# A hybrid decoder layer: the output products of an SSM pair are issued four steps after its first products

## The chip, the cores and the metric

The kernel runs on 1 core of one Trainium2 chip. The metric is the device time of one execution in microseconds (us), lower is better. Before the change the median of 3 runs is 755.06 us (754.26 to 757.27). The engines are named as the profile names them: PE is TensorE, DVE is VectorE, ACT is ScalarE, POOL is GpSimd, and SP is SyncE, which here only issues DMAs.

## What is computed

One layer on a sequence of 2048 rows of width 1024, in float32. The normalised input is multiplied with one matrix `w_in`, and three branches work on the columns of the result. A fourth set of columns gates them, and one more matrix closes the layer:

```python
h = rmsnorm(x, g_pre);  proj = h @ w_in
val, gate = proj[..., :MIX_W], proj[..., MIX_W:]
y_pool = pool_mixer(u_pool, w_pool, pool_scale)          # causal means over 2, 4, 8, 16 rows
y_ssm  = s5_mixer(u_ssm, a_re, a_im, log_dt, b_re, ...)   # 24 groups of 16 channels, 64 complex states each, then a gated unit
y_att  = memory_attention(q, mem, g_mem, w_kv)            # 4 heads into 256 memory tokens
y = concatenate([y_pool, y_ssm, y_att]) * silu(gate)
x = x + rmsnorm(y @ w_out, g_post)
```

The state-space mixer (SSM) is what the change is about. Its recurrence runs over time with a diagonal complex matrix. The kernel cuts time into 256 blocks of T = 8 rows: inside a block the output is a product with a small matrix, and from block to block a scan carries the state.

## The kernel before

Every float32 matrix product is made of three products of rounded parts: a value is split into a high part (an ACT copy to the rounded type) and a low part (a subtraction on DVE), and `mm3` (lines 162 to 165) issues high by high, high by low, low by high. `split` (lines 158 to 160) is the pair of ACT copy and DVE subtraction, so most splits carry line 159 or 160 in the profile.

**The phases.** First the input `x` is loaded transposed in four chunks of 512 rows, split, and multiplied with the SSM columns (tiles `pu`, written out as `us` to `ud`). Beside it run the keys and values of the memory (`pkv`, weights `wkv`), the tables of the SSM on POOL, the fold of the pooling weights (`pf`, `wpo`), and the row sums of squares of `x` (`rs_x`), from which a chain of small DVE instructions (`rs_sum` to the last `rs_y`) makes one scale per row. That scale is written to memory and read back as `rs_b` and `rs_ct`. Then come 52 projections, in two halves of the sequence: 13 weight tiles (2 queries `pjq`, 3 pooling `pjp`, 8 gates `pjg`) by 2 chunks in each half. Each is 24 matmuls of 128x512 into one of two banks of the tag `mm`. In the first half a weight tile of 1024x128 is loaded raw, split and also stored; in the second half the stored parts are loaded. Last come the gated unit (`pz`) and the output projection (`pout`).

**What sets the order.** The kernel is written in a tile language whose scheduler orders each engine's instructions by the program's order and by its own model of time. All engines then run their queues strictly in order. Work of the attention and of the SSM is cut into steps and put between projections: `tick_mid` (line 658) takes attention steps in the middle of a projection, `tick_end` takes one SSM step after each projection, at a pace of 1.02 steps. The 24 SSM groups are 12 pairs, and `ssm_schedule` (line 880) writes down the steps of each pair `b`, with `n = b + 1`:

```python
call((ssm_run1, b), (ssm_kernel_load, b), (ssm_build1, n))
call((ssm_kernel_split, b), (ssm_rotation, n))
call((ssm_input_load, n))
call((ssm_run2, b), (ssm_build2, n), (ssm_input_split, n), (ssm_output_split, n))
```

`ssm_run1` multiplies the split input `uh`, `ul` with `rh`, `rl` (tile `pa`) and takes the result through rotation and scan: `v`, `ax`, `gg`, `gs`, `h` alternate between ACT, DVE and POOL, and end in a split into `hh` (ACT) and `hl` (DVE). `ssm_run2` issues the output products: twelve matmuls into `py`, of `uh`, `ul` with `mh`, `ml` and of `hh`, `hl` with `oh`, `ol`. `ssm_build1` and `ssm_build2` make the matrices of the next pair (`ox`, `rt` on POOL; `pr` and `pk` on PE; `rh`, `rl`, `kst`). `ssm_kernel_load` reads `mraw` back from memory. The tiles `uh`, `ul`, `oh`, `ol`, `hh`, `hl` have one buffer each.

**Pools.** `t2k` (line 116) hands out temporaries of 2 KB per partition from 12 buffers; the row sums, the SSM steps and the attention use them. `w_tile` (line 586) loads a raw weight of 4 KB per partition into a buffer of its own, `wraw`, one in the pool `wp2` and, for two of the `wkv` weights, one in the pool of the first phase.

Of the kernel before, what the change touches and what calls it, by code (L numbers as in the profile page):

```python
# [10 lines left out]
F32 = mybir.dt.float32  # L11
F32R = mybir.dt.float32r
# [6 lines left out]
P = 128  # L19
D = 1024  # L20
SEQ = 2048
KT = D // P
# [11 lines left out]
NJ = SEQ // T  # L34
# [48 lines left out]
def hybrid_layer_kernel(  # L83
# [31 lines left out]
    def dma(o, i):  # L115
        nc.sync.dma_start(o, i)
# [11 lines left out]
    def t2k(name, shape=(P, CH), dtype=F32):  # L128
        return tmp.tile(list(shape), dtype, tag="t2k", name=name)
# [28 lines left out]
    def split(hi, lo, src, sub=dve):  # L158
        act.activation(hi, src, AF.Copy)  # L159
        sub.tensor_tensor(lo, src, hi.bitcast(F32), op=ALU.subtract)  # L160
# [122 lines left out]
    wp2 = p2.enter_context(tc.tile_pool(name="wp2", bufs=2, reuse_waits="tile"))  # L283
    p1 = ExitStack()
    ph1a = p1.enter_context(tc.tile_pool(name="ph1a", bufs=1))
# [247 lines left out]
    def mem_load():  # L533
        for k in range(KT):
            mr = xrp(f"mr{k}", (P, NMEM))
            dma(mr, memT[k * P:(k + 1) * P, :])
            m = big.tile([P, 2, NMEM], F32R, tag="xk", name=f"mhl{k}")
            act.activation(m[:, 0, :], mr, AF.Copy, scale=gmem[:, k:k + 1])
            dve.scalar_tensor_tensor(
                m[:, 1, :], mr, gmem[:, k:k + 1], m[:, 0, :].bitcast(F32), op0=ALU.mult, op1=ALU.subtract  # L540
            )
            mems.append(m)

    pkv = {}

    def kv_weight(m, raw=None):
        return w_tile(w_kv[:, m * P:(m + 1) * P], f"wkv{m}", raw)

    def kv_mm(m, w):
        if m % 2 == 0:  # L550
            pkv[m // 2] = mm_bank(f"pkv{m // 2}", (P, 2, NMEM))
        o = pkv[m // 2][:, m % 2, :]
        for k in range(KT):
            mm3(o, w[0][:, k, :], w[1][:, k, :], mems[k][:, 0, :], mems[k][:, 1, :], k == 0, k == KT - 1)
# [28 lines left out]
                dve.tensor_tensor(lo, src, hi.bitcast(F32), op=ALU.subtract)  # L583


    def w_tile(src, name, raw=None, spill=None, saved=None):
        wh = wp2.tile([P, KT, P], F32R, tag="whi", name=f"{name}_h")
        wl = wp2.tile([P, KT, P], F32R, tag="wlo", name=f"{name}_l")
        if saved is not None:
            dma(wh.bitcast(F32), saved[0])  # L590
            dma(wl.bitcast(F32), saved[1])
            return wh, wl
        wr = (raw or wp2).tile([P, KT, P], F32, tag="wraw", name=f"{name}_r", bufs=1)
        dma(wr, src.rearrange("(k p) m -> p k m", p=P))
        split(wh, wl, wr)
        if spill is not None:
            dma_later(spill[0], wh.bitcast(F32))
            dma_later(spill[1], wl.bitcast(F32))
        return wh, wl


    load_chunk(2, True)
    dma(gmem, g_mem)
    wkv = [kv_weight(0, ph1a)]
    mem_load()
    wkv.append(kv_weight(1))
    dma(cs, cst)
    u_mm(2, range(3), True)
    load_chunk(3, False)
    u_evac(2)  # L610
    kv_mm(0, wkv[0])
    wkv.append(kv_weight(2, ph1a))
    kv_mm(1, wkv[1])
    wkv.append(kv_weight(3))
    u_store(2)
# [48 lines left out]
    sp = ps_.enter_context(tc.tile_pool(name="sp", bufs=1, side="right", reuse_waits="tile"))  # L664
# [27 lines left out]
    def dma_later(o, i):  # L692

        deferred.append((o, i))
# [90 lines left out]
    def ssm_input_split(b, o):  # L785
        ur = o["ur"]
        pool.tensor_tensor(ur, ur, rs_ct.unsqueeze(1).broadcast_to([P, 2, NJ]), op=ALU.mult)
        uh = sp.tile([P, 2, NJ], F32R, tag="uh", name=f"uh{b}")
        ul = sp.tile([P, 2, NJ], F32R, tag="ul", name=f"ul{b}")
        split(uh, ul, ur)  # L790
        o["uh"], o["ul"] = uh, ul

# [85 lines left out]
    NB = NG // 2  # L878
    ssm_state = [dict() for _ in range(NB)]

    def ssm_schedule():
        def call(*fs):
            def go():
                for f, b in fs:
                    if b < NB:
                        f(b, ssm_state[b])

            ssm_q.append(go)

        call((ssm_input_load, 0), (ssm_build1, 0))  # L890
        call((ssm_build2, 0), (ssm_rotation, 0))
        call((ssm_input_split, 0), (ssm_output_split, 0))
        for b in range(NB):
            n = b + 1
            call((ssm_run1, b), (ssm_kernel_load, b), (ssm_build1, n))
            call((ssm_kernel_split, b), (ssm_rotation, n))
            call((ssm_input_load, n))
            call((ssm_run2, b), (ssm_build2, n), (ssm_input_split, n), (ssm_output_split, n))


    def q_split(ps, pr, c, qst):
# [346 lines left out]
    def prefetch(n):  # L1248
        if n < len(first_use) and first_use[n] not in weights:
            hf, i = first_use[n]  # L1250
            if hf not in tasks:
                tasks[hf] = half_tasks(hf)
            src, _, name = tasks[hf][i]
            if hf == 0:
                wsplit[i] = [dram.tile([P, KT, P], F32, name=f"ws{t}{i}") for t in "hl"]
                weights[hf, i] = w_tile(src, f"w{name}", spill=wsplit[i])
            else:
                weights[hf, i] = w_tile(src, f"w{name}", saved=wsplit[i])
# [15 lines left out]

    prefetch(0)
    ssm_schedule()
    for _ in range(3):
        ssm_q.popleft()()
# [3 lines left out]
    for n, (hf, i, cc) in enumerate(order):  # L1282
        if not (i == NTASK - 1 and cc == 0 or hf == 1 and i == 1 and cc == 0):
            prefetch(first_use.index((hf, i)) + 1)
        _, consume, name = tasks[hf][i]
# [121 lines left out]
```

## Time and profile before

| | before |
|---|---|
| median of 3 runs | 755.06 us (754.26 to 757.27) |
| the profiled execution | 754.54 us, of which the span from first to last instruction is 752.8 us |
| PE busy | 708.1 us, 94% of the span, 3449 matmuls |
| DVE busy | 525.7 us, 70% |
| ACT busy | 337.4 us, 45% |
| POOL busy | 364.1 us, 48% |
| granted TensorE clock, mean | 0.98 of 2.4 GHz |
| memory read and written | 81.68 MB and 38.68 MB |
| a load of half a row block of `x` (`rs_x`), or of one chunk piece (`xr`) | 256 KB, 32 of each |
| a raw projection weight (`wq_r`, `wp_r`, `wg_r`) | 512 KB, 13 of them |

PE has work in 94% of the span, so a gain must come from its idle time, from a higher granted clock, or from fewer matmuls. The change leaves the matmuls as they are. The table gives averages; which wait matters is read stage by stage.

### The profile page before, as it was taken

What the parts mean: (1) busy time and instruction counts of PE and PEld (TensorE: products, weight loads), DVE (VectorE), ACT (ScalarE), POOL (GpSimd) and SP (SyncE); (2) the same over time, 40 slices, a digit from 0 to 9 for tenths busy, and PEclk for the clock granted to TensorE, in tenths of its full rate; (3) what the DMA queues carried; (4) which work ended last, traced back from release to release, by engine and by line L of the source; (5) the groups of instructions that cost most, each with busy time, mean ns of one, the idle gap of its engine ahead of it and who ended that gap; (6) DMA issues with size and microseconds to landing.
All of it is one profiled execution on the core that took longest, in us unless ns stands there. A gap on an engine that the chain in (4) does not pass through costs nothing.

```text
span 752.8 us, 10077 instructions
## 1 busy us (share of the span) xinstructions
PE 708.1 (94%) x3449; PEld 575.9 (77%) x3449; DVE 525.7 (70%) x901; ACT 337.4 (45%) x731; POOL 364.1 (48%) x311
## 2 busy tenths in 40 slices
PE   6999787999979799888999999999999999999996
PEld 5788676887858588666888888888887888888885
DVE  4699594689889887978788978657606964343224
ACT  5675432557455453445555565447632524221111
POOL 0049852678758566846858488103042621421121
PEclk9999998999999899999999999999999999999999
DMA  7998985233333347482332324377725464330331
GB/s 252 309 328 270 336 288 156 98 108 126 121 114 119 112 150 247 161 280 83 122 107 71 121 81 154 134 224 275 226 80 192 130 199 123 113 126 14 112 113 56
DMA packets 95268, 121.03 MB, mean 161 GB/s; under 512 B 31585, under 2 KB 63025, under 8 KB 95217
## 3 DMA queue, kind: packets, MB, share of 16 engines
q1 hardware_dynamic: 82320, 90.08, 38.1%
q10 hardware_dynamic: 12896, 30.30, 10.6%
q8 instruction: 27, 0.44, 0.2%
q14 instruction: 25, 0.20, 0.1%
HBM read 81.68 MB, written 38.68 MB: 160 GB/s over the span
## 4 chain that ended last, share of the span: by engine, by line
PE 59%; DVE 13%; ACT 3%; issue 2%; DMA 1%; ACTq 0%; POOL 0%; DVEq 0%; POOLq 0%
PE pout L165 8%; PE pout L164 8%; PE pout L163 8%; PE pjg L163 5%; PE pjg L164 5%; PE pjg L165 5%; PE pz L163 2%; PE pz L165 2%; PE pz L164 2%; PE pjp L163 2%; PE pjp L164 2%; PE pjp L165 2%; DVE gg L847 2%; DMA ysd<-ys 1%; DVE yt L1007 1%
## 5 line engine op out<-in xcount | busy, mean ns | idle before, releaser
L163 PE MATMUL pjg<-xh,wg_h 128*128 128x512 f32 x256 | 103.6, 405 | 0.0
L164 PE MATMUL pout<-wol,yh 128*128 128x512 f32 (+1 forms) x264 | 102.0, 386 | 0.0
L164 PE MATMUL pjg<-xl,wg_h 128*128 128x512 f32 x256 | 101.9, 398 | 0.0
L165 PE MATMUL pjg<-xh,wg_l 128*128 128x512 f32 x256 | 101.7, 397 | 0.0
L163 PE MATMUL pout<-woh,yh 128*128 128x512 f32 (+1 forms) x264 | 101.6, 386 | 0.0
L165 PE MATMUL pout<-woh,yl 128*128 128x512 f32 (+1 forms) x264 | 101.2, 387 | 0.0
L1217 POOL TENSOR_TENSOR ov<-ov,xres 128x1024 f32<-128x1024 f32 x15 | 36.7, 2444 | 126.8 <-DVE ov L1216 105.0
L1213 ACT ACTIVATE ov<-pout 128x512 f32<-128x512 f32 x30 | 17.9, 596 | 105.3 <-PE pout L165 82.0
L163 PEld LDWEIGHTS pjg<-xh,wg_h 128*128 128x128 f32 x256 | 48.5, 189 | 12.8 <-issue 1.6
L164 PEld LDWEIGHTS pout<-wol,yh 128*128 128x128 f32 x264 | 49.5, 188 | 11.0
L163 PEld LDWEIGHTS pout<-woh,yh 128*128 128x128 f32 x264 | 49.5, 188 | 10.9
L165 PEld LDWEIGHTS pout<-woh,yl 128*128 128x128 f32 x264 | 49.5, 188 | 10.9
L165 PEld LDWEIGHTS pjg<-xh,wg_l 128*128 128x128 f32 x256 | 48.4, 189 | 11.3
L164 PEld LDWEIGHTS pjg<-xl,wg_h 128*128 128x128 f32 x256 | 48.7, 190 | 10.1
L160 POOL TENSOR_TENSOR yl<-yb,yh 128x512 fp32r<-128x512 f32 x20 | 26.9, 1375 | 60.6 <-ACT yh L159 39.7
L254 DVE SCALAR_TENSOR_TENSOR xl<-xr,gpre,xh 128x512 fp32r<-128x512 f32 x48 | 43.0, 908 | 18.7 <-ACT xh L253 18.6
L844 POOL TENSOR_TENSOR v<-v,ax 128x512 f32<-128x512 f32 x12 | 16.8, 1403 | 68.0 <-DVE ax L843 50.8
L253 ACT ACTIVATE xh<-xr,gpre 128x512 fp32r<-128x512 f32 x48 | 33.2, 715 | 32.4 <-DMA xr<-in_xT_dram 10.3
L163 PE MATMUL pu<-xh,wsh 128*128 128x512 f32 x96 | 39.0, 421 | 8.2 <-ACT wsh L159 6.8
L1185 DVE SCALAR_TENSOR_TENSOR ow<-ssq,ov 128x1 f32<-128x1 f32 x16 | 2.7, 168 | 54.7 <-ACT ov L1213 54.6
L163 PE MATMUL pjp<-xh,wp_h 128*128 128x512 f32 x96 | 39.0, 407 | 0.7 <-DVE gp L999 0.7
L164 PE MATMUL pu<-xl,wsh 128*128 128x512 f32 x96 | 38.7, 416 | 0.3 <-DVE xl L254 0.3
(300 smaller groups left out, 1929.3 us busy)
## 6 DMA issues: line engine op xcount, KB each, us to landing
xr<-in_xT_dram SPq DMA_DIRECT2D x32, 256.0 KB
rs_x<-in_x_dram SPq DMA_DIRECT2D x32, 256.0 KB
yd<-yt ACTq DMA_DIRECT2D x16, 512.0 KB
xres<-in_x_dram SPq DMA_DIRECT2D x16, 512.0 KB
out_dram<-ov SPq DMA_DIRECT2D x15, 512.0 KB
yb<-yd SPq DMA_DIRECT2D x20, 256.0 KB
wg_r<-in_w_in_dram SPq DMA_DIRECT2D x8, 512.0 KB
wsh<-wg_h ACTq DMA_DIRECT2D x8, 512.0 KB
```

The source lines that it names most:

```text
L160: sub.tensor_tensor(lo, src, hi.bitcast(F32), op=ALU.subtract)
L163: pe.matmul(ps, ahi, bhi, start=first, stop=False)
L164: pe.matmul(ps, ahi, blo, start=False, stop=False)
L165: pe.matmul(ps, alo, bhi, start=False, stop=last)
L253: act.activation(h, xr, AF.Copy, scale=gpre[:, k:k + 1])
L254: dve.scalar_tensor_tensor(l, xr, gpre[:, k:k + 1], h.bitcast(F32), op0=ALU.mult, op1=ALU.subtract)
L844: pool.tensor_tensor(v, v, ax, op=ALU.add)
L847: dve.tensor_tensor_scan(gg[:, i, :], r8[:, g0 + i:g0 + i + 1].broadcast_to([P, NJ]), v[:, i, :], 0.0, op0=ALU.mult, op1=ALU.add,)
L1007: dve.scalar_tensor_tensor(o, branch()[:, cc * CH:(cc + 1) * CH], 0.5, th, op0=ALU.mult, op1=ALU.mult)
L1185: dve.scalar_tensor_tensor(w, ssq[:, i:i + 1], 1.0 / D, v, op0=ALU.mult, op1=ALU.add)
L1213: act.activation(ov[:, HALVES[n]], ps[n], AF.Square, accum_out=ssq[:, n:n + 1])
L1217: pool.tensor_tensor(ov, ov, xr, op=ALU.add)
```

## The change

Four edits. The step `ssm_run2` of pair `b` moves from the fourth step of its pair into the first step of the next pair, ahead of that pair's own `ssm_run1`; `ssm_output_split` moves with it. `uh` and `ul` get a second buffer, because the input of pair `n` is now split while pair `b` still has to read its own. A raw weight is loaded and split in two halves of 256 KB, and these take buffers of `t2k` instead of `wraw`; this holds for the 4 weights `wkv` and the 13 projection weights of the first half. The private buffers `wraw` go.

```diff
-    def w_tile(src, name, raw=None, spill=None, saved=None):
+    def w_tile(src, name, spill=None, saved=None):
...
-        wr = (raw or wp2).tile([P, KT, P], F32, tag="wraw", name=f"{name}_r", bufs=1)
-        dma(wr, src.rearrange("(k p) m -> p k m", p=P))
-        split(wh, wl, wr)
+        for q in range(2):
+            ks = slice(q * KT // 2, (q + 1) * KT // 2)
+            wr = t2k(f"{name}_r{q}", (P, KT // 2, P))
+            dma(wr, src.rearrange("(k p) m -> p k m", p=P)[:, ks])
+            split(wh[:, ks], wl[:, ks], wr)
...
-        uh = sp.tile([P, 2, NJ], F32R, tag="uh", name=f"uh{b}")
-        ul = sp.tile([P, 2, NJ], F32R, tag="ul", name=f"ul{b}")
+        uh = sp.tile([P, 2, NJ], F32R, tag="uh", name=f"uh{b}", bufs=2)
+        ul = sp.tile([P, 2, NJ], F32R, tag="ul", name=f"ul{b}", bufs=2)
...
-                    if b < NB:
+                    if 0 <= b < NB:
...
-        call((ssm_input_split, 0), (ssm_output_split, 0))
-        for b in range(NB):
+        call((ssm_input_split, 0))
+        for b in range(NB + 1):
             n = b + 1
-            call((ssm_run1, b), (ssm_kernel_load, b), (ssm_build1, n))
+            call(
+                (ssm_run2, b - 1), (ssm_output_split, b), (ssm_run1, b), (ssm_kernel_load, b), (ssm_build1, n),
+            )
             call((ssm_kernel_split, b), (ssm_rotation, n))
             call((ssm_input_load, n))
-            call((ssm_run2, b), (ssm_build2, n), (ssm_input_split, n), (ssm_output_split, n))
+            call((ssm_build2, n), (ssm_input_split, n))
```

The scheduler turns this into new queues. Three places of them matter below.

PE, pair 2, before: the output products `py` stand between the scores `psc` of one attention step and the matrices of the next pair (`pr`, `pk`). `hl` is what DVE delivers last for them; `po` are the attention's values, `pa` the first products of pair 3.

```order
L920 MATMUL psc_1_1_1_2402<-kh,ql_0_1523 128x256
L163 MATMUL py_2452<-uh_2105,mh_2301 128x256
...
L163 MATMUL py_2452<-hh_2192,oh_2109 128x256
L164 MATMUL py_2452<-hl_2193,oh_2109 128x256
...
L165 MATMUL py_2452<-hh_2192,ol_2110 128x256
L745 MATMUL pr_2467<-ident,rt_2204 128x128 x2
...
L754 MATMUL pk_2474<-ox_2199,rt_2204 16x128 x2
...
L960 MATMUL po_1_0_2504<-pth_1_0_2385,vhl 128x256
...
L163 MATMUL pa_2547<-uh_2483,rh_2470 128x256
```

PE, pair 2, with the change (lines are shifted by 2 to 4):

```order
L924 MATMUL psc_1_1_1_2450<-kh,ql_0_1551 128x256
...
L747 MATMUL pr_2500<-ident,rt_2242 128x128 x2
L756 MATMUL pk_2507<-ox_2237,rt_2242 16x128 x2
...
L964 MATMUL po_1_0_2533<-pth_1_0_2433,vhl 128x256
...
L165 MATMUL pjp_0_1_2520<-xh_7_751,wp_0_l 128x512
L163 MATMUL py_2574<-uh_2130,mh_2345 128x256
...
L163 MATMUL py_2574<-hh_2230,oh_2201 128x256
L164 MATMUL py_2574<-hl_2231,oh_2201 128x256
...
L165 MATMUL py_2574<-hh_2230,ol_2202 128x256
L163 MATMUL pa_2593<-uh_2516,rh_2503 128x256
```

Between `psc` and `py` there now stand 27 matmuls of projections (10 before `pr`, 5 before `po`, 12 behind it), `pr`, `pk` and `po`, and `pa` of the next pair follows at once. The other pairs read alike, with 26 such matmuls or more.

SP, the raw weights `wq_0_r` of the first two projections, before: they are issued between the loads of the chunks of `x`.

```order
L116 DMA psc<-in_pool_scale_dram 96x384
L116 DMA wq_0_r<-in_w_in_dram 128x8x128
L116 DMA xr_5_516<-in_xT_dram 128x512
...
L116 DMA xr_4_715<-in_xT_dram 128x512
L116 DMA wq_0_r<-in_w_in_dram 128x8x128
L116 DMA xr_5_721<-in_xT_dram 128x512
...
L116 DMA rs_x_1_863<-in_x_dram 128x512
L116 DMA ur_1323<-ud 128x4x64 x2
L116 DMA wp_0_r<-wpd 128x8x128
L116 DMA rs_b_1293<-rsd 128x512
```

With the change they are issued behind the last load `rs_x`:

```order
L116 DMA rs_x_1_879<-in_x_dram 128x512
L116 DMA wq_0_r_1335<-in_w_in_dram 128x4x128
L116 DMA wq_0_r_1339<-in_w_in_dram 128x4x128
L116 DMA ur_1343<-ud 128x4x64 x2
L116 DMA wq_0_r_1393<-in_w_in_dram 128x4x128
L116 DMA wq_0_r_1397<-in_w_in_dram 128x4x128
L116 DMA rs_b_1309<-rsd 128x512
L116 DMA rs_b_1311<-rsd 128x512
```

Both weights of the queries moved past all 32 loads `rs_x`; `rs_b` stands behind all four halves.

DVE, the end of the row statistics and what follows, before:

```order
L195 SCALAR_TENSOR_TENSOR rs_x_1_863,ssq_x<-rs_x_1_863 128x512
L358 COPY wpo_1257<-pf_1252 128x384
L203 TENSOR_TENSOR rs_sum<-ssq_x 128x16
...
L179 SCALAR_TENSOR_TENSOR rs_y_1284<-rs_b_1282,rs_y_1278 128x16
L160 TENSOR_TENSOR ol_1370<-ox_1326,oh_1369 128x256
L160 TENSOR_TENSOR wp_0_l<-wp_0_r,wp_0_h 128x1024
L160 TENSOR_TENSOR rl_1342<-pr_1338,rh_1341 128x256
L904 TENSOR_TENSOR qf_0_1406<-pjq_0_0_1381,rs_b_1293 128x512
```

With the change:

```order
L195 SCALAR_TENSOR_TENSOR rs_x_1_879,ssq_x<-rs_x_1_879 128x512
L358 COPY wpo_1200<-pf_1195 128x384
L203 TENSOR_TENSOR rs_sum<-ssq_x 128x16
...
L179 SCALAR_TENSOR_TENSOR rs_y_1300<-rs_b_1298,rs_y_1294 128x16
L304 COPY us_1_1314<-pu_1_1219 128x64x8
L358 COPY wpo_1231<-pf_1226 128x384
...
L358 COPY wpo_1273<-pf_1268 128x384
L160 TENSOR_TENSOR wq_0_l<-wq_0_r_1335,wq_0_h 128x512
...
L160 TENSOR_TENSOR wq_0_l<-wq_0_r_1397,wq_0_h 128x512
...
L908 TENSOR_TENSOR qf_0_1426<-pjq_0_0_1401,rs_b_1309 128x512
```

The low halves `wq_0_l` of the first weights now stand behind the chain from `rs_sum` to `rs_y`, one copy `us` and four copies `wpo`; before, they were made long before, and all eight `wpo` stood ahead of the chain.

## Rows read from the trace of the kernel before

**Rows 1.** stretches: engines busy us (instructions), TensorE clock, DMA share, GB/s
```profile
0.00:123.40 123.40, 105.09 (x512) 86.48 (x512) 93.90 (x200) 62.97 (x123) 57.45 (x62) 0.97 0.86 283
123.40:350.50 227.10, 209.63 (x1045) 167.77 (x1046) 191.96 (x241) 113.94 (x251) 154.98 (x133) 0.96 0.44 147
350.50:516.00 165.50, 165.50 (x890) 136.44 (x889) 125.80 (x185) 89.33 (x214) 88.19 (x83) 1.00 0.39 125
```

**Rows 2.** waits of PE from 123.4 to 350.5: us in total, times, longest
```profile
PE py L164 <- DVE hl L160: 10.6, 5, 3.9
PE pjq L163 <- DVE qf L904: 3.9, 1, 3.9
PE py L163 <- ACT hh L159: 3.1, 2, 2.3
```

**Rows 3.** timeline of PE: start, duration, work [idle before it and what ended it]
```profile
215.96 0.38 PE L163 MATMUL py<-hh,oh 128*128 128x256 f32 x1 [2.32 <-ACT hh L159]
217.86 0.39 PE L164 MATMUL py<-hl,oh 128*128 128x256 f32 x1 [1.52 <-DVE hl L160]
...
250.91 0.38 PE L163 MATMUL py<-hh,oh 128*128 128x256 f32 x1 [0.76 <-ACT hh L159]
255.16 0.58 PE L164 MATMUL py<-hl,oh 128*128 128x256 f32 x1 [3.86 <-DVE hl L160]
```

**Rows 4.** timeline of DVE around the wait of pair 2
```profile
217.12 0.68 DVE L160 TENSOR_TENSOR hl<-h,hh 128x512 fp32r<-128x512 f32 x1
...
218.90 1.29 DVE L160 TENSOR_TENSOR ptl<-ptp,pth 128x512 fp32r<-128x512 f32 x2
```

**Rows 5.** stretches from one wait to the next, columns as in Rows 1
```profile
182.50:217.86 35.36, 30.80 (x170) 24.84 (x170) 30.72 (x41) 18.27 (x46) 27.77 (x24) 1.00 0.31 102
217.86:255.16 37.30, 32.67 (x174) 26.49 (x174) 33.34 (x42) 20.05 (x49) 27.40 (x21) 0.92 0.32 107
255.16:287.00 31.84, 31.84 (x156) 26.08 (x156) 26.43 (x37) 16.32 (x37) 17.48 (x16) 0.94 0.53 169
```

**Rows 6.** five microseconds around the longest wait, columns as in Rows 1
```profile
250.00:255.00 5.00, 0.54 (x3) 0.19 (x1) 4.94 (x5) 2.55 (x5) 4.80 (x4) 0.73 0.31 114
```

**Rows 7.** groups of DVE by form: busy us, mean ns of one, idle before
```profile
L160 DVE TENSOR_TENSOR hl<-h,hh 128x512 fp32r<-128x512 f32 x12 | 13.2, 1104 | 1.1 <-ACT hh L159 1.1
L160 DVE TENSOR_TENSOR wg_l<-wg_r,wg_h 128x1024 fp32r<-128x1024 f32 x8 | 12.2, 1526 | 0.2 <-ACT wg_h L159 0.2
...
L304 DVE COPY us<-pu 128x512 f32<-128x512 f32 x6 | 6.2, 1064 | 0.1
...
L358 DVE COPY wpo<-pf 128x384 f32<-128x384 f32 x8 | 4.4, 548 | 0.0
```

**Rows 8.** timeline of PE at the first projections
```profile
107.14 0.50 PE L163 MATMUL pjq<-xh,wq_h 128*128 128x512 f32 x1 [1.61 <-DVE wpo L358]
...
123.39 0.80 PE L163 MATMUL pjq<-xh,wq_h 128*128 128x512 f32 x1 [3.92 <-DVE qf L904]
```

**Rows 9.** timeline of DVE at the row statistics of x
```profile
89.40 0.67 DVE L480 SCALAR_TENSOR_TENSOR rd<-ph 128x492 f32<-128x492 f32 x1 [4.94 <-POOL ph L479]
...
115.06 0.17 DVE L179 SCALAR_TENSOR_TENSOR rs_y<-rs_b,rs_y 128x16 f32<-128x16 f32 x1
...
122.64 0.69 DVE L904 TENSOR_TENSOR qf<-pjq,rs_b 128x512 f32<-128x512 f32 x1 [1.00 <-DMA rs_b<-rsd]
```

**Rows 10.** timeline of SP (issues): second projection weight, last loads of x
```profile
57.38 0.38 SPq L116 DMA_DIRECT2D wq_r<-in_w_in_dram  x1
...
83.64 14.69 SPq L116 DMA_DIRECT2D rs_x<-in_x_dram  x18
```

**Rows 11.** waits of SP from 123 to 300, columns as in Rows 2
```profile
SPq L116 <- DVE gg L847: 19.9, 3, 7.6
```

**Rows 12.** timeline of ACT and PE at the first gated product
```profile
507.53 1.13 ACT L1119 ACTIVATE ge<-yr 128x512 f32<-128x512 f32 x1
...
515.55 0.39 PE L163 MATMUL pz<-gh,wgh 128*128 128x512 f32 x1
```

More of the change, by code (lines that the diff above doesn't have):

```diff
@@ L544, in hybrid_layer_kernel, with kv_weight @@
     pkv = {}
-    def kv_weight(m, raw=None):
-        return w_tile(w_kv[:, m * P:(m + 1) * P], f"wkv{m}", raw)
+    def kv_weight(m):
+        return w_tile(w_kv[:, m * P:(m + 1) * P], f"wkv{m}")
     def kv_mm(m, w):
@@ L603, in hybrid_layer_kernel @@
     dma(gmem, g_mem)
-    wkv = [kv_weight(0, ph1a)]
+    wkv = [kv_weight(0)]
     mem_load()
@@ L611, in hybrid_layer_kernel @@
     kv_mm(0, wkv[0])
-    wkv.append(kv_weight(2, ph1a))
+    wkv.append(kv_weight(2))
     kv_mm(1, wkv[1])
```

## Prediction

> **What bounds the kernel now.** I read the stretches of the span first. PE is busy throughout from 350.5 to 516 at a clock of 1.00, so nothing is to be won there. It idles 227.10 - 209.63 = 17.5 us between 123.4 and 350.5, at a mean clock of 0.96, and 18.3 us in the first 123.4 us [rows 1]. These are the two places to look at.
>
> The waits of PE name the first place: the output products `py` wait 10.6 us for `hl` from DVE in 5 waits and 3.1 us for `hh` from ACT in 2 [rows 2]. That is 13.7 of the 17.5 us. Another 3.9 us is the third projection's wait for `qf`, which belongs to the first place of the other kind, below. The timeline shows the four longest waits of `py`: 2.32 and 1.52 us in pair 2, 0.76 and 3.86 us in pair 3, 8.46 us together [rows 3]. PE's queue is in order, so projections that need nothing from `hl` stand behind `py`.
>
> Why is `hl` late? DVE is late as a whole: it makes `hl` at 217.12, and the splits `ptl` of an attention step, which PE needs soon after, follow only at 218.90 [rows 4]. Over the two stretches that end in these waits DVE is busy 30.72 + 33.34 = 64.06 us of 72.66, PE 30.80 + 32.67 = 63.47, part of it at a clock of 0.92 [rows 5]. So PE and DVE are nearly level there, and DVE lags by some microseconds.
>
> The first 123.4 us end differently. The first projection starts at 107.14, and the third waits until 123.39 [rows 8], because its bank is evacuated with `rs_b`, which comes from the chain of row statistics. That chain ends at 115.06 + 0.17 = 115.23 us on DVE, and `qf` follows at 122.64 [rows 9]. So what ends this stage is the chain, not PE.
>
> **The sum, part by part**, against the profiled execution's own 754.54 us, which lies 0.5 us under the median of 755.06.
>
> *The moved products.* By the order, 26 or more projection matmuls now run between the place where `py` waited and its new place. 48 such matmuls, with a few small ones, took from 107.14 to 123.39 - 3.92 = 119.47, so 0.26 us each [rows 8]; 26 of them are 6.8 us. The longest sum of waits in one pair is 0.76 + 3.86 = 4.62 us [rows 3]. If `hl` is not later than now, all of them are covered: -13.7 us.
>
> *What is late next.* DVE's work stays, so its lag shows elsewhere: at `po`, which needs `ptl`, and at a projection that needs its bank. Without the 8.46 us PE would need 64.2 us for the two stretches and DVE has 64.06 us of work in them, all of it in order and with idle time of its own (8.6 us now) [rows 5]. Bounds: it gives back nothing, if the lag is carried into the next stretch, where DVE has 31.84 - 26.43 = 5.4 us free; it gives back all 8.46 us, if DVE cannot run denser than now. I take 3 us, nearer the lower end, as the 5.4 us free stand right behind.
>
> *The halves.* A low part of 128x1024 takes DVE 1526 ns in the mean, one of 128x512 1104 ns where it stands among the same neighbours [rows 7], so a weight costs DVE up to 0.7 us more. ACT pays a similar extra, but it is busy half of the stretch at most [rows 1]. For four weights in the two dense stretches that is under 3 us and lies within the 3 us taken above.
>
> *The clock.* It stood at 0.92 and 0.94 in the stretches of and after the longest wait [rows 5]: 0.08 x 37.3 + 0.06 x 31.84 = 4.9 us. Of this 0.27 x 5 = 1.35 us fell where PE had nothing to do [rows 6], so at most 3.5 us come back, and nothing if DVE sets the pace. Ahead of the low reading PE had idled 3.86 us [rows 3]. I take -2 us, about the share of the stretch behind the wait, where DVE has room.
>
> *The first weights.* They now arrive behind the loads `rs_x`, and their low halves stand on DVE behind the chain, one `us` (1.06 us), four `wpo` (0.55 us each) and the first half itself (about 0.9): the first projection starts 4.2 us after the chain's end, and the third 12.3 us later [rows 7, 8]. Before, the third started 123.39 - 115.23 = 8.2 us after the chain's end. So this costs 16.5 - 8.2 = 8.3 us if the chain ends when it does now, and it gains if the chain is over 8.3 us earlier. It will be earlier. Two weights of 512 KB no longer stand ahead of the loads; 18 loads of 256 KB were issued in 14.69 us [rows 10], 0.82 us each, so 4 x 0.82 = 3.3 us at least. On DVE the stall of 4.94 us ahead of `rd` [rows 9] is overtaken by loads that now stand ahead of it, five `wpo` (2.7 us) and two low parts (1.53 us each) go behind the start of the chain: 10.7 us at most. So +5.0 to -2.4 us; I take 7 us earlier, the middle, and +1.3 us. What covers the late weights is the chain itself; without it all of the 4.2 us would be bare.
>
> *The tail.* The last matmul of the last pair's `py` moves 24 matmuls later, 6.2 us by the measure above. On ACT it holds the gated unit's weights and the first `ge`, at 507.53; the first `pz` starts at 515.55 [rows 12]. After `ge` come its split on ACT and DVE, some 2 us, so about 6 us were free. +0.5 us, between 0 and 2.
>
> *The rest at nothing.* The 17 extra DMA issues cost SP under 0.4 us each [rows 10], beside transfers that PE does not wait for [rows 2]; `ol` of a pair now comes one step later and POOL's `ox` waits for it, but the two other factors of `ox` and `rt` follow only after `v`. Without that cover the wait of POOL would reach `pr`.
>
> Sum: 754.54 - 13.7 + 3 - 2 + 1.3 + 0.5 = 743.6 us.
>
> **The rivals.**
>
> *DVE sets the pace.* The waits move from `py` to `po` and the banks. For it: DVE is busy 0.87 and 0.89 of the two stretches [rows 5]. Against it: the stretch behind has 5.4 us free. Then 8.46 us come back and the clock gives nothing: 754.54 - 13.7 + 8.46 + 1.3 + 0.5 = 751.1 us.
>
> *All of it comes.* Nothing is given back, the clock returns 3.5 us, the chain ends 10.7 us earlier: 754.54 - 13.7 - 3.5 - 2.4 = 734.9 us. Against it: it needs DVE without its own idle time.
>
> *Slower: the halves arrive late.* A half now needs a free buffer of `t2k`, which a late DVE instruction releases, and SP's queue is in order. SP already waits for such a release, `gg`, 3 times for 19.9 us, 6.6 us each [rows 11]. A weight is fetched one task, 48 matmuls or 12.3 us, ahead; take off two loads (1.6 us) and the splits behind others (about 4 us), and 6.7 us are left. If both halves of a weight wait 6.6 us one after the other, PE stands 13.2 - 6.7 = 6.5 us. For three weights, as often as SP waits for `gg` now, that is 19.5 us: 743.6 + 19.5 = 763 us. It decides from 6.7 us of waiting per weight on. Against it: in the stretch PE never waits for a raw weight now [rows 2].
>
> Beside it the Trainium skill (DMA: Bandwidth & Descriptors, the sections on the anatomy of one DMA and on rules for kernel authors) speaks against halving: it puts about 2 us of fixed cost on every DMA and asks for large transfers. By that estimate the four first halves, one behind the other, would take 4 x 2 = 8 us longer and the sum would be about 751 us. The trace differs for loads in a row: 0.82 us per 256 KB [rows 10], which is what the sum uses.
>
> *It does not do what it says.* The scheduler could put `hl` later by as much as `py`. In the changed order `hl` still stands ahead of the same `ptl`, so I give this little: about 755 us.
>
> **How the numbers follow.** A difference under 0.5%, 3.8 us, can hardly be told from none by this measurement, so faster means under 751.3. The forecast, with its bounds some 738 to 749, gets 0.50; all of it 0.12; DVE sets the pace 0.18, of which nearly half falls under 751.3; no effect 0.06; slower 0.14. Faster: 0.50 + 0.12 + 0.08 = 0.70. Within: 0.10 + 0.06 = 0.16. Slower: 0.14. The range goes from 734, just under the case in which all comes, to 757, which leaves out most of the slower case.
>
> **What would show it.** Right: no wait of PE for `hl` or `hh` over 0.5 us in the first half; PE's idle time between the third projection and the reload of `x` under 7 us; the clock near 1.00 in the stretch of pair 3; the chain's end near 108 and the third projection near 125. DVE at over 0.92 with new waits of `po` or of `pjp` and `pjg` for evacuations would show the first rival, waits of `pjp` or `pjg` for `wp_l`, `wg_l` or a raw DMA the slower one. The prediction is wrong if `py` still waits, or if the third projection starts after 128.

## The result and the profile after

The changed kernel takes 784.62 us in the median (784.12 to 785.77, 4 runs) against 756.16 us (754.26 to 757.83, 4 runs): a ratio of 1.0383, interval 1.0356 to 1.0409. It is **slower by some 29 us**, where I had forecast 743.6 us. The profiled execution of after took 784.34 us, its span 782.5. One execution of a run below, c1, took 2043.32 us and is left out of its time; as it is the one that was profiled, no view of c1 is used.

The time is found by cutting both spans at the same points of the work: the start of the first pool projection, the start of the seventh (the first of the second half), and the start of the first gated product. The two profiles have 1013 matmuls recorded in the second of these stretches. Before, then after, stretches with the columns of [rows 1]:

```profile
0.00:139.20 139.20, 120.89 (x577) 99.20 (x578) 101.36 (x210) 66.65 (x129) 59.75 (x64) 0.95 0.80 262
139.20:355.70 216.50, 199.03 (x1013) 159.22 (x1012) 187.99 (x239) 114.23 (x258) 153.88 (x134) 0.97 0.45 148
355.70:515.60 159.90, 159.90 (x855) 131.95 (x855) 122.06 (x176) 84.96 (x202) 87.00 (x79) 1.00 0.40 127
515.60:752.80 237.20, 228.23 (x1009) 185.52 (x1007) 114.30 (x277) 71.61 (x146) 63.47 (x35) 1.00 0.41 135
```

```profile
0.00:152.70 152.70, 126.01 (x581) 101.75 (x581) 103.82 (x223) 72.15 (x149) 67.10 (x73) 0.91 0.71 234
152.70:383.40 230.70, 207.16 (x1013) 162.92 (x1013) 191.27 (x243) 112.79 (x259) 138.57 (x124) 0.93 0.42 143
383.40:542.60 159.20, 159.20 (x850) 131.15 (x849) 114.73 (x174) 81.70 (x194) 87.26 (x80) 1.00 0.38 126
542.60:782.50 239.90, 229.01 (x1009) 185.22 (x1008) 113.37 (x278) 74.78 (x149) 63.23 (x35) 0.99 0.42 135
```

The start loses 152.7 - 139.2 = 13.5 us, the rest of the first half with the turn to the second 230.7 - 216.5 = 14.2, the steady part -0.7, the end 2.7: together 29.7, the whole difference of the spans. In the two losing stretches PE stands idle more (8.4 us and 6.1 us: length less busy time), and its mean clock falls from 0.95 to 0.91 and from 0.97 to 0.93, which is a larger share of the time at the lower of its two levels. The rest of the 27.7 us is PE busy for longer (5.1 and 8.1 us), in the second stretch on as many matmuls.

The waits of PE over the whole span of after (engine, line, what ended the wait: us in total, times, longest):

```profile
PE pjq L164 <- DVE xl L254: 5.9, 6, 2.6
...
PE ptp L953 <- ACT pex L942: 5.3, 3, 3.2
...
PE pjp L165 <- DVE wp_l L160: 4.6, 2, 3.1
PE pjg L163 <- ACT wg_h L159: 3.5, 1, 3.5
PE pjg L165 <- DVE wg_l L160: 3.5, 1, 3.5
PE pjq L163 <- ACT wq_h L159: 2.6, 1, 2.6
...
PE pjp L163 <- ACT wp_h L159: 2.3, 1, 2.3
```

No row names `py` any more: the 13.7 us of [rows 2] are gone, as forecast. In their place PE waits for the raw weights' splits, `wq`, `wp` and `wg`, for which it never waited before: 13.9 us for `wp` and `wg`. The waits for `xl` at the turn to the second half (0.6 us before) and for the attention's `pex` (none before) come on top.

**The start.** PE, ACT and SP (issues) of after, timeline rows as in [rows 3]:

```profile
113.20 0.38 PE L227 MATMUL rs_t<-ident,rs_y 128*16 128x128 f32 x1 [5.70 <-DVE rs_y L179]
114.52 3.73 PE L356 MATMUL pf<-wp,wpt 96*128 96x96 f32 x16 [0.93 <-DVE wpo L358]
120.89 0.79 PE L163 MATMUL pjq<-xh,wq_h 128*128 128x512 f32 x1 [2.64 <-ACT wq_h L159]
```

```profile
117.17 2.04 ACTq L119 DMA_DIRECT2D wpd<-wpo  x2
119.30 0.39 ACTq L119 DMA_DIRECT2D rsd<-rs_o  x1
...
120.20 1.68 ACT L159 ACTIVATE wq_h<-wq_r 128x512 fp32r<-128x512 f32 x3 [4.46 <-issue]
```

```profile
98.45 1.81 SPq L116 DMA_DIRECT2D wq_r<-in_w_in_dram  x2
...
108.27 0.92 SPq L116 DMA_DIRECT2D wq_r<-in_w_in_dram  x2
```

The query weights are fetched at 98 and 108 us instead of 43 and 57 ([rows 10] has the second), behind all loads of the squares. So their splits come last in ACT's queue, behind the stores of the fold and of the row statistics; and `rs_t` now stands ahead of the last fold matmuls on PE, which wait for the end of the statistics with it. What ran beside the chain now follows it.

**The pairs.** The third pool weight, on SP (issues, then the wait ahead of them), ACT and PE of after:

```profile
206.59 1.16 SPq L116 DMA_DIRECT2D mraw<-kd  x2
207.85 2.98 SPq L116 DMA_DIRECT2D wp_r<-wpd  x2
```

```profile
SPq L116 <- DMA kd<-kst: 19.2, 1, 19.2
```

```profile
216.82 0.63 ACT L837 ACTIVATE gs<-gg 64x512 f32<-64x512 f32 x1 [7.06 <-DVE gg L849]
...
221.19 0.62 ACT L159 ACTIVATE wp_h<-wp_r 128x512 fp32r<-128x512 f32 x1
```

```profile
221.86 0.79 PE L163 MATMUL pjp<-xh,wp_h 128*128 128x512 f32 x1 [2.34 <-ACT wp_h L159]
...
227.36 0.80 PE L165 MATMUL pjp<-xh,wp_l 128*128 128x512 f32 x1 [3.08 <-DVE wp_l L160]
```

Before, the same weight was fetched at 177.48 and used at 203.8, 26 us later. Now its halves go out at 207.85 and 210.45 for a use at 221.9. They stand on SP behind the reload `mraw`, which waits 19.2 us until the products `kd` that it reads are stored. They land within 3.2 us, and still ACT splits the first of them only at 221.19: in order, it first waits 7.06 us for `gg` and does the attention's `pex`. Over the whole span ACT waits for the landing of a raw projection weight only once:

```profile
ACT wg_h L159 <- DMA wg_r<-in_w_in_dram: 0.3, 1, 0.3
```

So what PE waits for in the pairs is the place of the splits in the queues of ACT and DVE, more than the landing of the halves.

### The profile page after: what moved, and what is told of

Read it like the earlier page. It is cut to its first block, busy times and chain, and to the rows that moved or that the text cites. A ratio compares the mean times of both kernels' runs of the same rounds, so it can differ in the third digit from the quotient of the medians.

```text
span 782.5 us, 10130 instructions
## 1 busy us (share of the span) xinstructions
PE 721.4 (92%) x3449; PEld 581.0 (74%) x3449; DVE 523.2 (67%) x918; ACT 341.4 (44%) x748; POOL 356.2 (46%) x311
## 4 chain that ended last, share of the span: by engine, by line
PE 47%; DVE 5%; DMA 3%; issue 2%; ACT 1%; POOL 0%; DVEq 0%; ACTq 0%; SPq 0%
PE pout L165 7%; PE pout L164 7%; PE pout L163 7%; PE pjg L163 4%; PE pjg L165 4%; PE pjg L164 4%; PE pz L163 2%; PE pz L164 2%; PE pz L165 2%; PE pjp L163 1%; PE pjp L165 1%; DVE xl L254 1%; DMA yr<-ysd 1%; PE pjp L164 1%; DMA xr<-in_xT_dram 1%
## 5 line engine op out<-in xcount | busy, mean ns | idle before, releaser
L165 PE MATMUL pjp<-xh,wp_l 128*128 128x512 f32 x96 | 40.1, 418 | 4.7 <-DVE wp_l L160 4.6
L164 PE MATMUL pjp<-xl,wp_h 128*128 128x512 f32 x96 | 39.5, 412 | 0.0
```

Source lines behind the costliest of these rows:

```text
L164: pe.matmul(ps, ahi, blo, start=False, stop=False)
L165: pe.matmul(ps, alo, bhi, start=False, stop=last)
```

## Experiments

The differences in us below are the ratio less one, times 755. In each edit `-` is the kernel that the label starts from. The skip terms by pair, for room in several runs, are one edit: the table `ddg` of all 24 groups goes, and each pair makes its own of 16x32 on POOL.

### The halves, where they lie

w1_halves_in_temporaries, from the kernel before:

```diff
-        wr = (raw or wp2).tile([P, KT, P], F32, tag="wraw", name=f"{name}_r", bufs=1)
+        for q in range(2):
+            wr = t2k(f"{name}_r{q}", (P, KT // 2, P))
...
```

and w2_halves_own_buffers, from w1:

```diff
-            wr = t2k(f"{name}_r{q}", (P, KT // 2, P))
+            wr = wp2.tile([P, KT // 2, P], F32, tag="wraw", name=f"{name}_r{q}", bufs=2)
```

> The kernel before with the raw weights alone changed: two halves each, taken from the temporaries; the output products stay where they were. Theory A (taking raw halves from the temporaries ties each load to the release of an older temporary and puts its splits late in the queues of ScalarE and VectorE; the moved products are not to blame): the first projection starts near 121 us instead of 107.1, raw weights are waited for again in the pairs, and the output products still wait for their low parts: 780 to 797 us. Theory B (the moved products cost the 14 us between the first pool projection and the seventh): only the start is late, 768 to 772 us. Theory C (the cut in two costs, wherever the halves lie): as A, 780 or more.

> The kernel before with raw weights in two halves, in two buffers of their own of the same total size as the one whole buffer was. Theory A: the first projection starts at 107 us or a little later, no raw weight is waited for, 752 to 760 us. Theory C: the doubled loads and splits cost their share here too, 770 us or more. Theory B says nothing on the halves: about 756 us.

w1: 775.25 us, ratio 1.0283 (1.0261 to 1.0306), 21 us slower. w2: 758.72 us, 1.0059 (1.0039 to 1.0078), 4.5 us slower. So the halves cost 4.5 us in buffers of their own, and that they are temporaries costs 17 more. w1 came out below what I expected of it by 5 us, since its first projection starts at 116.4 and not near 121 (the reason is in the last section). Its waits of PE on raw weights, 140 to 345 us:

```profile
PE pjg L165 <- DVE wg_l L160: 4.3, 1, 4.3
PE pjp L165 <- DVE wp_l L160: 4.3, 2, 3.3
...
PE pjp L163 <- ACT wp_h L159: 2.9, 2, 1.6
```

In w2 there is none. There SP waits for the splits of the weight before, and that is early enough. Its 4.5 us are not all shown to come from the cut: 2.5 us of them are lost before the first pool projection (141.75 instead of 139.22). There PE waits 2.3 us for the splits of `wkv`, whose halves share the same two buffers, and 5.1 us for `qf` instead of 3.9, as one DVE step of the row statistics takes 6.36 us in this profile (last section).

### The start apart

h1_first_weights_whole, from the changed kernel (with the skip terms by pair): `wkv` and `wq` whole and in `wraw` as before, the other weights in halves from `t2k`.

> The changed kernel with the weights of keys, values and queries whole and in buffers of their own, as before the change; the twelve or so pool and gate weights of the first half in halves from the temporaries, as changed. Skip terms by pair, for room. If the late start comes from the query weights' halves standing in line behind the tiles of the squares (theory A): first projection at 107 us, and 768 to 773 us: the 12 to 14 us of the start come back, those of the pairs stay, with waits on wp and wg. If the start is late for another reason: 780 us or more. If the waits in the pairs only follow from the late start: 750 to 760 us.

776.67 us, 1.0281 (1.0249 to 1.0312). The first projection starts at 106.84, so the late start is the query weights' place behind the squares (h1 gives `wkv` its buffers back as well, but it is `wq_h` that PE waits for in the changed kernel). But 8 us come back, not 12 to 14: the first pool projection still starts 7 us late, at 146.4. Its weight is now the first among the temporaries. The halves land at 130, ACT splits them at 145.68, behind `gg` and the attention's `pex`; and on PE the attention's `ptp`, which came behind the first pool projection before, now stands ahead of it and waits for that `pex` (whole span):

```profile
PE ptp L958 <- ACT pex L947: 9.0, 3, 6.4
```

### What holds the halves back

q1_kernels_by_act_queue, from the changed kernel:

```diff
-            dma(mr[:, i, :], bass.AP(kd.tensor, ...))
+            store(mr[:, i, :], bass.AP(kd.tensor, ...))
```

> The changed kernel, but the reloads of the pairs' kernel products (mraw, two per pair) are issued by ScalarE's queue instead of SP's. In the changed kernel SP stands up to 19 us (91.3 us in six waits) at these reloads, and a weight's two halves come right behind them. If that order in SP's queue is what makes the halves late: wp's third pair of halves is issued over 15 us ahead of its use as before, the waits on wp and wg (10.8 us between 186 and 323 us) are gone, 770 to 775 us. If the halves are late because their slots of the temporaries come free late: the wait on SP moves to the halves themselves, the waits of TensorE stay, 782 to 788 us.

782.07 us, 1.0335 (1.0308 to 1.0362). The reloads no longer stand ahead of the weight on SP, and yet its halves go out only 2 us earlier. SP now waits for the slot itself, whose last reader is the attention's `attn` (timeline, then a wait of SP from 183 to 215):

```profile
205.78 4.74 SPq L116 DMA_DIRECT2D wp_r<-wpd  x2
```

```profile
SPq L116 <- DVE attn L973: 18.1, 1, 18.1
```

So the order of SP's queue alone is refuted as the cause: without it, the slot holds the issue almost as long.

a1_kernels_out_of_temporaries, from the changed kernel with the skip terms by pair:

```diff
-        mr = o["mr"] = t2k(f"mraw{b}", (P, 2, P))
+        mr = o["mr"] = sp.tile([P, 2, P], F32, tag="mraw", name=f"mraw{b}", bufs=2)
```

> The changed kernel with the kernel products' reload (1 KB, which takes a temporary of 2 KB) in two buffers of its own, so that the temporaries carry one tile less in every pair; skip terms by pair, for room. If the ring of temporaries is what holds the halves back, each half's slot comes free a little earlier: 776 to 782 us. If SP's order holds them: 783 to 787 us.

781.59 us, 1.0336 (1.0317 to 1.0356): some 3.5 us less than the changed kernel, the upper end of what the ring's theory expected. q1 gave as much, so the time does not tell the two theories apart. One temporary fewer per pair brings the third pool weight's halves out at 202.69, 5 us earlier, and yet ACT splits them at 219.48, again behind `gg`:

```profile
219.48 1.16 ACT L159 ACTIVATE wp_h<-wp_r 128x512 fp32r<-128x512 f32 x2
```

PE waits 5.1 us for `wp_h` in this profile, against 2.3 us. Earlier halves do not help as long as their splits stand that late.

e1_same_memory_split, from the changed kernel:

```diff
-    EV, NTMP = 4, 16
+    EV, NTMP = 4, 14
-            wr = t2k(f"{name}_r{q}", (P, KT // 2, P))
+            wr = wp2.tile([P, KT // 2, P], F32, tag="wraw", name=f"{name}_r{q}", bufs=2)
```

> The changed kernel with the same memory divided otherwise: 10 temporaries, and two buffers of 2 KB for the raw halves alone, instead of 12 temporaries for all. If the halves are late because they take their turn behind older temporaries, the own buffers win although 4 KB fewer are left to the rest: 766 to 778 us, no wait for wp or wg. If the kernel is simply short of buffers (11 temporaries cost 7 to 9 us before the change): 780 to 790 us, waits of TensorE for other work instead.

768.58 us, 1.0166 (1.0128 to 1.0204): 16 us less than the changed kernel out of the same memory. PE waits for no `wq`, `wp` or `wg` of the first half. The third pool weight goes out at 189.06, ahead of `mraw` on SP, and is split at 201.15 for a use at 217.44. So it is the turn in the common ring, not the number of buffers: with it the scheduler puts the issue behind `mraw` and the splits behind `gg`. Which of the two places costs how much is not shown.

### The moved products

c1_eleven_temporaries and m1_moved_whole_raw. Whole raw weights in their own buffer and two pairs' split inputs don't fit together with 12 temporaries, so both have `NTMP = 15`; m1 is otherwise the changed kernel without the halves.

> The kernel before with 11 temporaries instead of 12: what the memory for the run with the moved products costs by itself. All theories: 754 to 760 us; more would have to be taken off the run with the moved products.

> The changed kernel with whole raw weights in the buffer of their own again; output products moved and split inputs of two pairs held, as changed. To fit, the pool of temporaries has 11 instead of 12. Theory A: the first projection starts at about 107 us, the waits of the output products are gone, 742 to 750 us. Theory B: the start is as before, but the pairs lose 14 us, 766 to 772 us. Theory C: 742 to 750 us.

c1: 761.47 us in the median of three, 1.0113 (1.0085 to 1.0141). m1: 765.06 us, 1.0141 (1.0104 to 1.0178). c1 is above what I expected; m1 comes near theory B's range, but by c1 8.5 of its 10.6 us go with the missing temporary. One temporary is worth 8.5 us in the kernel before, and beside that the move gains nothing. To have it without this loss, the skip terms by pair make room:

m2_moved_alone is the changed kernel without the halves, with 12 temporaries; c2_skip_terms_by_pair is the kernel before with the edit that makes the room.

> The moved output products and the split inputs of two pairs alone: whole raw weights in the buffer of their own, 12 temporaries, all as before. Room for it comes from the table of skip terms (16 partitions, 1.5 KB), which GpSimd now makes pair by pair. Theory A, as I had it in the prediction (the stalls on the low parts of the state disappear): the first projection starts at 107 us, 742 to 747 us. Theory D (VectorE sets the pace between 180 and 265 us; the wait only moves to the next instruction that needs it, the kernel products pk and the attention's): some of 8 us of waits come back at pk, 749 to 757 us, none of them at the output products.

> The kernel before with the skip terms made pair by pair: the control of the run with the moved products alone. Both theories: 752 to 757 us, no difference that can be told.

c2: 755.5 us, 1.0006 (0.9990 to 1.0022). m2: 762.21 us, 1.0081 (1.0049 to 1.0114), **slower** by 6 us, beyond both theories. Stretches, c2 and then m2, from the first pool projection on; the second row lies inside the first:

```profile
139.70:314.60 174.90, 164.50 (x847) 133.04 (x845) 150.52 (x193) 94.29 (x217) 129.16 (x116) 0.95 0.41 135
184.00:265.00 81.00, 72.15 (x368) 57.62 (x367) 68.94 (x91) 42.55 (x108) 55.45 (x48) 0.90 0.32 109
314.60:357.90 43.30, 37.07 (x168) 27.87 (x168) 39.07 (x47) 20.06 (x41) 26.61 (x26) 0.96 0.58 198
357.90:755.20 397.30, 388.29 (x1862) 317.33 (x1861) 230.34 (x453) 156.95 (x347) 151.42 (x117) 0.99 0.40 132
```

```profile
140.10:314.60 174.50, 162.88 (x843) 129.77 (x841) 155.33 (x192) 95.03 (x218) 125.53 (x117) 0.98 0.41 135
184.00:265.00 81.00, 72.59 (x378) 57.21 (x379) 74.22 (x95) 41.98 (x104) 52.26 (x45) 0.96 0.38 128
314.60:362.60 48.00, 40.12 (x175) 30.39 (x175) 39.92 (x49) 21.56 (x45) 24.56 (x24) 0.89 0.53 179
362.60:761.50 398.90, 388.31 (x1858) 316.33 (x1856) 230.19 (x452) 156.36 (x342) 152.36 (x118) 1.00 0.40 131
```

To the start of the last gate output of the first half (314.6 in both) the move gives 0.4 us. The clock does come back there, 0.95 to 0.98, but PE idles 11.6 us instead of 10.4, and DVE is busy 74.22 of 81 us where it had been 68.94, and PE waits for it all the same. At the turn to the second half 4.7 us are lost, behind it 1.6. In the turn PE idles 7.9 us instead of 6.2 and its clock is 0.89 instead of 0.96; part of the 4.7 us is order, as all six products `pa` of a pair now stand ahead of the first pool projection and not one. The waits of PE in m2 (whole span) name the successors of `hl` (`pk`, `po`) and, at the turn, the reloads:

```profile
PE pk L747 <- DVE attn L971: 8.5, 3, 4.4
...
PE pjq L165 <- DMA wq_l<-wsl: 2.9, 2, 2.5
PE pjq L164 <- DVE xl L254: 2.5, 3, 1.3
PE pjq L163 <- DMA wq_h<-wsh: 2.5, 1, 2.5
PE po L962 <- DVE ptl L160: 1.7, 1, 1.7
```

m4_moved_low_reload_apart, from m2, and c4_low_reload_apart, from the kernel before, try the loss at the turn. In m2 the reload of `wq_l` had come to stand on SP behind a piece of `x` that waits for `xl`.

```diff
-            dma(wl.bitcast(F32), saved[1])
+            (store if name[:2] == "wq" else dma)(wl.bitcast(F32), saved[1])
```

> The run with the moved products alone, but the low parts of the two query weights are reloaded for the second half by ScalarE's queue, so that they don't stand in SP's queue behind a piece of the input that waits for VectorE (320.17 us there, 5.8 us of wait). If that place in the queue is what the moved products lose at the start of the second half: TensorE's waits on the two query weights (5.4 us) shrink to 2 us or less and the time is 756 to 759 us. If VectorE sets the pace there too: 760 to 764 us, the waits going to the low parts of x. If the moved products gain anything where nothing else is in the way: below 752 us.

> The kernel before with the same reload on ScalarE's queue: the control. Its waits on the two query weights are 1.9 us, so 753 to 757 us.

m4: 762.65 us, 1.0085 (1.0058 to 1.0113). c4: 754.46 us, 0.9979 (0.9961 to 0.9997). That place in the queue is not the cause; the wait on `wq_l` is gone, and one for `wq_h`, whose reload is issued at 329.34 behind another waiting piece of `x`, takes its place:

```profile
PE pjq L163 <- DMA wq_h<-wsh: 5.6, 1, 5.6
```

In this profile a DVE operation of 8.04 us (last section) falls just ahead of the turn as well. So what makes the turn to the second half longer after the move stays open beyond these waits.

### Both parts, and a try for more

m3_moved_halves_own: the changed kernel with the raw halves in two buffers of their own (as in w2) and the skip terms by pair.

> The changed kernel with the raw halves in two buffers of their own instead of the temporaries (skip terms by pair, for room): moved products and split loads together, without the shared pool. If the parts add up (moved alone +6.6, halves in own buffers +4.7): 764 to 769 us. If moved products only cost where weights come late: 755 to 762 us.

765.09 us, 1.0115 (1.0095 to 1.0134), 9 us: a little under the 4.5 + 6 of its parts. The same sum for the change itself is w1 + m2, 21 + 6 = 27 us, against 29 measured.

b1_small_tiles_own: the kernel before with skip terms by pair, `mraw` in two and `kst` in one buffer of `sp`.

> The kernel before with the reloads of the kernel products and their staging tile in buffers of their own, so that two temporaries of 2 KB fewer are taken in every pair. If the count of temporaries is a limit of the kernel before too (11 instead of 12 cost 9 us): 746 to 754 us. If 12 are enough: 753 to 757 us.

760.94 us, 1.0064 (1.0046 to 1.0081). More room among the temporaries, and 5 us slower: `py` then waits 4.7 us for `mh` and `ml`. That the loss with 11 temporaries is one of count is therefore not shown. No version beats the kernel before by more than c4's 0.2%.

## Why the prediction was wrong

- **The step that failed is "the halves": costed at under 3 us and put inside another term.** I counted the work of the splits alone. Measured: 4.5 us for halves in buffers of their own (w2) and 17 us for where the halves lie (w1 less w2). A tile taken from `t2k` waits until a reader gives one of the twelve shared buffers back, so a weight, needed at a fixed time, takes its turn behind attention and SSM temporaries that DVE is late with; and in that turn its splits stand late in ACT's and DVE's queues, which is what PE waits for.
- **"The halves arrive late", my slower rival at 763 us,** had the place and the release of a slot. Its price was too small: I took waits of 6.6 us per half [rows 11]; the third pool weight waits 18.1 us for one slot in q1. And it took PE to wait for the landing, where a1 and ACT's single wait of 0.3 us show the place of the splits. It also left out the query weights, and the clock that falls after the waits.
- **The first weights (+1.3 us, bounds -2.4 to +5.0): measured +13.5 at the first pool projection.** I had the load order and the low halves on DVE. I missed ACT, whose splits of the high halves stand behind the fold's stores, and PE, where `rs_t` had moved ahead of the last fold matmuls. The first projection comes 120.89 - 113.15 = 7.7 us after the chain's end, not 4.2, and the chain ended at 113, not at 108. In w1, with the same order there, it ended at 108.66. The third projection, which I had put near 125 with 128 as the sign of being wrong, needs a bank that the first `qf` empties only at 131.69 + 0.69 = 132.4 us.
- **The moved products (-13.7 us):** the `py` waits went, as I said. **"What is late next" (+3 us)** was the wrong choice between its bounds: in m2 the whole 8.46 us and more come back, at `pk` and `po`. The argument that the lag is carried into the stretch behind, where DVE has time, failed, because `pk` stands ahead of that stretch and waits for `attn` on DVE (by the code, for one of the six small PSUM banks, which `attn` empties). So DVE sets the pace there, the rival at 751.1 us. The 8.46 us were also no upper bound: I called the four waits of pairs 2 and 3 the longest, but one in pair 4 of the kernel before is longer than two of them:

```profile
316.52 0.38 PE L164 MATMUL py<-hl,oh 128*128 128x256 f32 x1 [2.70 <-DVE hl L160]
```

- **The clock (-2 us)** was too small where only the move is made: 0.90 to 0.96 over 81 us in m2, 0.06 x 81 = 4.9 us. It does not help as long as DVE sets the pace.
- **The tail (+0.5 us, bounds 0 to 2):** 2.7 us in the changed kernel, a size missed.
- **Not in the prediction at all:** the turn to the second half, 4.7 us in m2.
- By the estimate from the Trainium skill's fixed cost per DMA (DMA: Bandwidth & Descriptors, the section on the anatomy of one DMA) halving was to cost 8 us. That section gives its figure for DMAs that GpSimd issues, while SP issues these, and of the four halves only two are DMAs more than before. w2 measured 4.5 us, but from the first pool projection on PE waits there for no raw weight, so they are not shown to be that cost; and the other 17 us are no cost of a transfer.

## What to carry to other kernels

A load that must be early needs a buffer whose last reader is early; out of the same memory, two buffers of its own were 16 us better than a turn among twelve shared ones. Cost such a change by asking which instruction releases the slot and where the work on the loaded tile then stands in its queues, not how long the load takes. And a stall removed from one engine's queue is a gain only if the engine that it waited for has time free before the next point that needs it.

## What the chip showed that I had not expected

DVE's short operations depend on what POOL does beside them. The same step of the row statistics, 128x16, in the changed kernel, with the POOL operation beside it, and in w1, where POOL stands idle from 106.75 to 113.84:

```profile
111.33 1.19 DVE L179 SCALAR_TENSOR_TENSOR rs_y<-rs_b,rs_y 128x16 f32<-128x16 f32 x1
```

```profile
111.21 1.28 POOL L824 TENSOR_TENSOR ss<-ss,tr 128x512 f32<-128x512 f32 x1
```

```profile
107.86 0.17 DVE L179 SCALAR_TENSOR_TENSOR rs_y<-rs_b,rs_y 128x16 f32<-128x16 f32 x1
```

The chain of statistics, from `rs_v` on, takes 104.24 to 113.15 us there against 104.55 to 108.66 in w1: that is the 4.5 us by which w1 started earlier. It can be far more than the length of one POOL operation: in w2 one of these 128x16 steps takes 6.36 us. In m4 one DVE operation that takes 0.68 us elsewhere takes 8.04 us, while POOL runs seven from 309.24 on, one directly behind the other (first and last of them shown):

```profile
309.23 8.04 DVE L1009 SCALAR_TENSOR_TENSOR yt<-attn,th 128x512 f32<-128x512 f32 x1
```

```profile
309.24 0.95 POOL L723 TENSOR_TENSOR rt<-rt,cmbr 128x256 f32<-128x256 f32 x1
...
316.10 0.64 POOL L721 TENSOR_TENSOR rt<-Bre,XT__113 128x256 f32<-128x256 f32 x1
```

The Trainium skill (SBUF — State Buffer, "SBUF: two separate sides") has VectorE with two inputs from SBUF and GpSimd share a port that one of them holds for a whole instruction. The rows agree that one waits for the other. They go beyond it in that, as the profile has it, DVE got no turn between seven instructions of POOL. That the port is the cause is argued from the overlap; no run took POOL's work away.
